# Eight of the 22 blocks of half 1's first feed-forward moved from beside half 0 to the head of half 1's own course

## The chip, the cores and the metric

One core of a Trainium2 chip runs the whole program. The time is device time in microseconds of one execution, as the median of several. A core has TensorE (PE, with its weight loads shown apart as PEld), VectorE (DVE), ScalarE (ACT), GpSimd (POOL) and SyncE (SP, which issues most DMAs here). Each engine takes its instructions in the order in which the program gives them to it.

## The reference, cut to what matters

Three transformer blocks follow each other on x of 512 tokens by 1024 channels, all in float32. What the change touches is the first step of the first block and the experts of the second:

```python
def first_block(x, ...):
    x = layer_norm(ALPHA * x + 0.5 * swiglu(x, ffn1_w_gate, ffn1_w_up, ffn1_w_down), ln1_g, ln1_b)
    # mixer: projections of x, HGRN2 over chunks, a causal convolution of width 31, output projection
    x = layer_norm(ALPHA * x + mix, ln2_g, ln2_b)
    x = layer_norm(ALPHA * x + 0.5 * swiglu(x, ffn2_w_gate, ffn2_w_up, ffn2_w_down), ln3_g, ln3_b)

def swiglu(x, w_gate, w_up, w_down):            # 1024 -> 2816 -> 1024
    return (silu(x @ w_gate) * (x @ w_up)) @ w_down

def second_block(x, ...):
    # mixer: spatial gating and a gated delta rule (a triangular solve per chunk of 64)
    ids, gates = peer_routing(h, wq, keys1, keys2)      # 8 heads x 16 experts for each token
    act = gelu(einsum('pd,phkd->phk', h, expert_u[ids]))
    x = x + gate * einsum('phk,phkd->pd', gates * act, expert_v[ids])
```

The third block (retention, a state space mixer and a feed-forward) comes last. The sequence is causal in the mixers, so tokens 256 to 511 need states of tokens 0 to 255, but not the other way round.

## The kernel before, in words

The tokens are worked on as two halves of 256 (`hf` 0 and 1, each two tiles of 128 tokens, `X(t)`). The program is written as one long course in which other work is mixed by hand.

- **Head** (`all`): half 0 goes through block 1 and the mixer of block 2 (`block1_first`, `layer_norm`, `block1_rest`, `mix2`). Here a weight tile (128x1024, 512 KB) is loaded by SP into `wr`, split by ACT (`wH`, L226) and DVE (`wL`, L227) into two parts, and each product is made of three matmuls. **Beside it runs the aside**: half 1's first feed-forward, a generator (`g_block1_first`), with its own tiles `fr`, `fH`, `fL` and `hH`, `hL`. Wherever the foreground is expected to leave PE without work it calls `idle(d)` with a fixed `GAP`, and pieces of the generator are issued for that long. `ASIDE1 = (4, 4, 4, 4, 4, 2)` says into how many parts its 22 blocks of 128 hidden channels are cut; a part of 4 takes 8 tiles of gate and up and 4 of down, one of 2 takes 4 and 2. `drain_side` issues what is left behind half 0's mixer.
- **Experts** (`experts`): now `exact` is true, a weight tile is used as it is in float32, and each product is one matmul (two records in the trace). `peer_route` makes half 0's expert ids, and its gathers go into the list `fill`: 512 steps that each fetch 128 rows of 4 KB by an indirect DMA of POOL (L1188) into one of 15 buffers `gu`; DVE makes a dot product of each row of `peer_u` (L1195), and a weighted sum of those of `peer_v` (L1218) that PE takes over in part (L1212). Some steps of the routing are in the list too. In front of this runs half 1's own course: `layer_norm` ln1, `block1_rest` (mixer 1 with hgrn and the convolution, ln2, second feed-forward, ln3) and `mix2`. Then half 1 is routed, and its gathers run beside half 0's block 3.
- **Tail** (`end`): half 1's block 3, with the rest of half 0's as aside.

How many gathers are issued beside the foreground is set by credit: each weight tile and each PSUM tile calls `tick(d, load)`, which adds `d * z * rate - load`, and a step is issued when its price (`DMA = 1.46` for a gather) is there. `z` is the first number of the stage's `ZONE`, the second (`vshare`) is the share of the weighted sums that PE takes. `course` sets the rate for a whole course from two fixed sums. At the second routing the list is emptied.

A float32 tile of the gate in this stage is issued so:

```python
raw = self.weight(self.wp, "w", 6 if self.exact else 4, src)      # wtile, L220: the DMA on SP
...
nc.tensor.matmul(ps[:, i * TH:(i + 1) * TH], a[:, k * P:(k + 1) * P], b[:, k, :], ...)   # g_fm, L280
```

`transpose_x` (L334) brings x into the layout that the matmuls take (`XH`, and `XL` when split); the down product is `g_tm` (L302 in float32, L304 to L306 split), whose result DVE adds to X (L390). In the delta recurrence of `mix2` a triangular inverse is built in steps: L1010 (PE), L1012 (ACT copy), L1016 and L1019 (PE), L1021 and L1022 (DVE subtractions).

Of the kernel before, what the change touches and what calls it, by code (L numbers as in the profile page):

```python
# [11 lines left out]
F32 = mybir.dt.float32  # L12
# [7 lines left out]
P = 128  # L20
T = 512
NT = 4
NH = 2
TH = 256
D = 1024
# [10 lines left out]
DMA, ROUTE, FINISH = 1.46, 0.8, 6.0  # L36
AHEAD = 8
GB = 15

ASIDE1 = (4, 4, 4, 4, 4, 2)  # L40
ASIDE3 = (4,) * 4
FIRST3 = 16
ADA = 28
CONV_PE = (0, 2)

ZONE = dict(x=(1, 0.5), g=(1, 0.35), h=(1.15, 0.41), c=(0.43, 0.4), f=(1.43, 0), m=(1.73, 0.06), d=(1.09, 0.4),
            R=(1.09, 0.39), r=(1.33, 0.3), F3=(1.1, 0), s=(1, 0.65))

GAP = dict(_0=4, l=3, h=0.74, c=0.22, m=5.53, d=0.9, r=0.5, s=1.6, _4=5.2, ln=8, l4=8)
# [1 line left out]
WEIGHTS = 3  # L51
# [26 lines left out]
class Ker:  # L78
# [68 lines left out]
    def course(self, i):  # L147

        whole, loads, share = COURSE[i]
        self.rate, self.credit = (share * sum(f[0] for f in self.fill) + loads) / whole, 0.0  # L150

    def tick(self, d, load=0.0):
# [11 lines left out]
    def zone(self, name):  # L164
        self.z, self.vshare = ZONE[name]

# [300 lines left out]
    def g_block1_first(self, parts):  # L467
        nc = self.nc
        yield from self.g_transpose_x(lambda t, k: self.X(t)[:, k * P:(k + 1) * P])
        for t in range(NH):  # L470
            self.aux.tensor_scalar(self.X(t), self.X(t), float(ALPHA), None, op0=ALU.mult)
        yield from self.g_ffn_glu("f1g", "f1u", "f1d", parts)

    def block1_rest(self):
        self.zone("g")
        self.mixer1()
        self.zone("f")
        self.layer_norm("ln2_g", "ln2_b", ALPHA)
        if self.hf == 0:
            self.fill, self.rate, self.credit = self.later, RATE_ADA[1], 0.0  # L480
        with self.tc.tile_pool(name="ada", bufs=1) as self.adap:
            self.ffn_glu("f2g", "f2u", "f2d", (22,))
            self.pop(9999 if self.hf == 0 else 0)
        self.layer_norm_out("ln3_g", "ln3_b")
# [1316 lines left out]
    def all(self, out):  # L1801
        tc = self.tc
        self.load_x()
        with ExitStack() as ef:
            self.wp = ef.enter_context(tc.tile_pool(name="wp", bufs=1))
            self.ff0 = ef.enter_context(tc.tile_pool(name="aside", bufs=1))
            with ExitStack() as es:
                self.xt(es)
                self.ff = self.ff0
                self.aside(1, lambda o: o.g_block1_first(ASIDE1))  # L1810
                ada = self.ada_setup()
# [20 lines left out]
    def experts(self, out):  # L1832


        tc = self.tc
        with ExitStack() as ep:
            self.exact = True
            self.wp = ep.enter_context(tc.tile_pool(name="wp", bufs=1))
            self.peer_open(ep)
            self.zone("x")  # L1840
            self.fill = []
            self.peer_route(RATE_ROUTE[0])
            self.course(0)
            self.hf = 1
            with ExitStack() as es:
                self.xt(es)
                self.layer_norm("ln1_g", "ln1_b", ALPHA)
                self.block1_rest()
            self.mix2()
            self.zone("R")  # L1850
            self.peer_route(RATE_ROUTE[1])
            self.course(1)
            self.hf = 0
            last = self.ctx.enter_context(ExitStack())
            with ExitStack() as es:
                self.xt(es)
                self.block3_mix()
                X = self.XH, self.XL
                self.exact = False
                self.xt(last, "right")  # L1860
                X3 = self.XH, self.XL
                self.exact = True
                self.XH, self.XL = X
                self.zone("F3")
                self.whole(self.g_norm3())
                for i in range(0, KD, 2):
                    i = slice(None), slice(i, i + 2)
                    self.fill_pair(self.XH[i], self.cut(X3, *i))
                self.whole(self.g_ffn_relu2((FIRST3,)))
            self.exact = False  # L1870
            self.XH, self.XL = X3
            self.rate = 0.0
            self.ff = last.enter_context(tc.tile_pool(name="aside3", bufs=1, side="right"))
            self.aside(0, lambda o: o.g_block3_last(out, ASIDE3, FIRST3), False)
            self.aux = self.nc.gpsimd
            self.next_piece()
            self.pop(9999)
# [149 lines left out]
```

## Time and profile before

| | us |
|---|---|
| median of 3 runs | 3463.89 (3454.16 to 3475.46) |
| the profiled execution | 3472.09 |
| its span, first to last instruction | 3470.3 |

| engine | busy us | share of the span |
|---|---|---|
| PE | 3035.7 | 87% |
| DVE | 2661.0 | 77% |
| POOL | 1437.0 | 41% |
| ACT | 1152.0 | 33% |

In all 956.97 MB are moved, 276 GB/s in the mean. The shares are averages over three quite different stretches: the head reaches to about 908 us, the experts from there to about 2896 us, the tail from there to the end. The mean granted clock of TensorE is 0.932 of full speed.

### The profile page before, as it was taken

What the parts mean: (1) busy time and instruction counts of PE and PEld (TensorE: products, weight loads), DVE (VectorE), ACT (ScalarE), POOL (GpSimd) and SP (SyncE); (2) the same over time, 40 slices, a digit from 0 to 9 for tenths busy, and PEclk for the clock granted to TensorE, in tenths of its full rate; (3) what the DMA queues carried; (4) which work ended last, traced back from release to release, by engine and by line L of the source; (5) the groups of instructions that cost most, each with busy time, mean ns of one, the idle gap of its engine ahead of it and who ended that gap; (6) DMA issues with size and microseconds to landing.
All of it is one profiled execution on the core that took longest, in us unless ns stands there. A gap on an engine that the chain in (4) does not pass through costs nothing. (4 is left out here: it accounts for less than half of the span.)

```text
span 3470.3 us, 44861 instructions
## 1 busy us (share of the span) xinstructions
PE 3035.7 (87%) x15418; PEld 2355.2 (68%) x15418; DVE 2661.0 (77%) x6451; ACT 1152.0 (33%) x1694; POOL 1437.0 (41%) x1187
## 2 busy tenths in 40 slices
PE   9999999998979789988677859798888975999998
PEld 9987889888866458846354644465644644888897
DVE  7779676665488999779898989898778776566655
ACT  4454544553312242103122121122222213455554
POOL 0020000023245656656677567667677671211200
PEclk9999999999989899998788979898899987999999
DMA  8863476542389979998989889999999995644364
GB/s 313 283 193 116 135 266 228 169 157 85 110 297 363 342 290 382 409 396 348 374 319 377 324 324 401 327 382 351 334 363 361 409 390 186 185 131 138 122 188 162
DMA packets 276469, 956.97 MB, mean 276 GB/s; under 512 B 38272, under 2 KB 41856, under 8 KB 276240
## 3 DMA queue, kind: packets, MB, share of 16 engines
q0 software_dynamic: 147456, 536.94, 40.9%
q1 hardware_dynamic: 128784, 417.16, 35.0%
q8 instruction: 122, 2.00, 0.2%
q14 instruction: 107, 0.88, 0.1%
HBM read 947.68 MB, written 2.10 MB: 274 GB/s over the span
## 5 line engine op out<-in xcount | busy, mean ns | idle before, releaser
L1188 POOL DMA_INDIRECT gu<-in_peer_u,idx x512 | 614.6, 1200 | 368.0 <-issue 114.1
L1188 POOL DMA_INDIRECT gu<-in_peer_v,idx x512 | 627.5, 1226 | 306.1 <-issue 112.3
L1195 DVE SCALAR_TENSOR_TENSOR gu<-gu 128x1024 f32<-128x1024 f32 x512 | 622.1, 1220 | 61.5 <-DMA gu<-in_peer_u,idx 60.7
L227 DVE TENSOR_TENSOR wL<-wr,wH 128x1024 fp32r<-128x1024 f32 x332 | 409.2, 1235 | 251.1 <-ACT wH L226 231.9
L280 PE MATMUL ps<-XH,wr 128*128 128x256 f32 x2368 | 535.8, 386 | 0.0
L280 PEld LDWEIGHTS ps<-XH,wr 128*128 128x128 f32 x2368 | 454.8, 194 | 72.1 <-issue 11.5
L226 ACT CAST wH<-wr 128x1024 fp32r<-128x1024 f32 x332 | 348.7, 1051 | 448.4 <-PE ps L305 219.5
L1218 DVE SCALAR_TENSOR_TENSOR gu<-gu,act 128x1024 f32<-128x1024 f32 x362 | 463.5, 1280 | 27.3 <-DMA gu<-in_peer_v,idx 21.6
L1212 PE MATMUL ps<-gu,dg 128*128 128x512 f32 x584 | 318.7, 672 | 95.1 <-DMA gu<-in_peer_v,idx 43.0
L1212 PEld LDWEIGHTS ps<-gu,dg 128*128 128x128 f32 x584 | 117.6, 214 | 212.5 <-issue 150.9
L302 PE MATMUL ps<-wr,XH 128*128 128x512 f32 x512 | 230.2, 602 | 0.0
L280 PE MATMUL ps<-XH,wH 128*128 128x256 f32 x1408 | 208.1, 290 | 13.2 <-ACT XH L138 11.2
L280 PE MATMUL ps<-XH,wL 128*128 128x256 f32 x1408 | 202.7, 288 | 3.2 <-DVE wL L227 3.0
L280 PE MATMUL ps<-XL,wH 128*128 128x256 f32 x1408 | 202.8, 288 | 0.2
L280 PEld LDWEIGHTS ps<-XH,wH 128*128 128x128 f32 x1408 | 187.9, 197 | 19.1 <-ACT XH L138 15.3
L280 PEld LDWEIGHTS ps<-XH,wL 128*128 128x128 f32 x1408 | 186.1, 196 | 4.7 <-DVE wL L227 4.6
L227 DVE TENSOR_TENSOR fL<-fr,fH 128x1024 fp32r<-128x1024 f32 x98 | 127.1, 1298 | 79.4 <-ACT fH L226 48.6
L280 PEld LDWEIGHTS ps<-XL,wH 128*128 128x128 f32 x1408 | 186.4, 197 | 0.6 <-DVE XL L140 0.6
L302 PEld LDWEIGHTS ps<-wr,XH 128*128 128x128 f32 x512 | 97.9, 194 | 121.5 <-issue 119.1
L226 ACT CAST fH<-fr 128x1024 fp32r<-128x1024 f32 x98 | 102.7, 1049 | 183.6 <-PE ps L280 57.7
L302 PE MATMUL ps<-wr,hH 128*128 128x512 f32 x304 | 135.4, 607 | 18.1 <-DVE xres L390 13.0
L208 POOL TENSOR_TENSOR r<-rx,mhalf 128x1 f32<-128x1 f32 x18 | 11.9, 668 | 335.9 <-DVE rx L206 332.5
(619 smaller groups left out, 5391.1 us busy)
## 6 DMA issues: line engine op xcount, KB each, us to landing
wr<-in_wi_fm SPq DMA_DIRECT2D x112, 512.0 KB
wr<-in_wi_tm SPq DMA_DIRECT2D x96, 512.0 KB
wr<-in_wf SPq DMA_DIRECT2D x96, 512.0 KB
wr<-in_wo SPq DMA_DIRECT2D x64, 512.0 KB
wa<-in_wada SPq DMA_DIRECT2D x48, 512.0 KB
wr<-in_f2g SPq DMA_DIRECT2D x44, 512.0 KB
wr<-in_f2u SPq DMA_DIRECT2D x44, 512.0 KB
wr<-in_f2d SPq DMA_DIRECT2D x44, 512.0 KB
```

Of the source, the lines that this page charges most:

```text
L208: nc.gpsimd.tensor_tensor(out=out, in0=x, in1=self.mhalf[:p, :].to_broadcast(list(out.shape)), op=ALU.pow)
L226: self.nc.scalar.copy(H, raw)
L227: self.nc.vector.tensor_tensor(out=L, in0=raw, in1=H, op=ALU.subtract)
L280: nc.tensor.matmul(ps[:, i * TH:(i + 1) * TH], a[:, k * P:(k + 1) * P], b[:, k, :], start=n == 0, stop=n == KD * len(terms) - 1)
L302: nc.tensor.matmul(pss[t], lh[:, ts], wh, start=k == 0, stop=k == nk - 1)
L1188: nc.gpsimd.indirect_dma_start(out=g, out_offset=None, in_=I[src], in_offset=bass.IndirectOffsetOnAxis(ap=idx[:, s:s + 1], axis=0))
L1195: nc.vector.scalar_tensor_tensor(g, g, 1.0, h2, op0=ALU.mult, op1=ALU.mult, accum_out=st["act"][:, s:s + 1])
L1212: nc.tensor.matmul(st["ps"][i], dg, g[:, i * 512:(i + 1) * 512], start="pe" not in st, stop=s == 127)
L1218: nc.vector.scalar_tensor_tensor(st["acc"], g, c, st["acc"], op0=ALU.mult, op1=ALU.add)
```

## The change

`ASIDE1` becomes `(4, 4, 4, 2)`: the aside makes 14 of half 1's 22 blocks. The other eight are made in one part at the head of half 1's course, ahead of ln1, in float32 as it is there and with the gathers beside them; the new zone `f1` has the numbers of the second feed-forward's. As the transposed x of half 1 is gone by then, x is fetched a second time and transposed again. The rate of the course is worked out with the added tiles.

```diff
-ASIDE1 = (4, 4, 4, 4, 4, 2)
+ASIDE1 = (4, 4, 4, 2)
...
+ZONE = dict(f1=(1.43, 0), x=(1, 0.5), g=(1, 0.35), h=(1.15, 0.41), c=(0.43, 0.4), f=(1.43, 0), ...
...
     def course(self, i):
         whole, loads, share = COURSE[i]
+        n = 2 * (FIRST3 - 16) if i else 3 * (22 - sum(ASIDE1))
+        whole, loads = whole + n * WEIGHTS, loads + n * DMA
         self.rate, self.credit = (share * sum(f[0] for f in self.fill) + loads) / whole, 0.0
...
+    def block1_more(self):
+        fb = sum(ASIDE1)
+        if fb == 22:
+            return
+        self.zone("f1")
+        with self.tc.tile_pool(name="xin", bufs=1) as xp:
+            xi = xp.tile([P, NH, D], F32, name="xi")
+            for t in range(NH):
+                self.nc.sync.dma_start(xi[:, t, :], self.I["x"][self.tg(t) * P:(self.tg(t) + 1) * P, :])
+            self.transpose_x(lambda t, k: xi[:, t, k * P:(k + 1) * P])
+        self.ffn_glu("f1g", "f1u", "f1d", (22 - fb,), fb)
+        self.zone("x")
...
                 self.xt(es)
+                self.block1_more()
                 self.layer_norm("ln1_g", "ln1_b", ALPHA)
                 self.block1_rest()
```

With `FIRST3 = 16` the rate of the second course stays as it is.

## Rows read from the trace of the kernel before

**Rows 1.** Busy time of the engines by stretch: PE, PEld, DVE, ACT, POOL, clock, DMA.

```profile
772.30:908.30 136.00, 124.23 (x919) 115.42 (x919) 74.20 (x109) 56.26 (x76) 40.41 (x30) 0.97 0.27 86
...
794.50:829.70 35.20, 34.99 (x258) 33.13 (x259) 18.12 (x25) 11.87 (x15) 6.38 (x5) 0.95 0.25 81
...
860.20:894.70 34.50, 34.50 (x247) 32.31 (x248) 17.15 (x21) 11.97 (x15) 6.44 (x5) 0.96 0.27 80
...
1125.00:1232.00 107.00, 82.10 (x303) 45.53 (x301) 101.31 (x307) 23.60 (x44) 73.47 (x64) 0.90 0.94 346
...
1448.00:1533.00 85.00, 79.94 (x225) 42.91 (x224) 56.09 (x131) 6.00 (x9) 50.99 (x42) 0.98 1.03 409
...
1693.00:1852.00 159.00, 111.61 (x559) 78.19 (x559) 146.43 (x291) 37.22 (x65) 114.30 (x96) 0.83 0.91 327
```

**Rows 2.** The same by stretch for tile fr alone: DVE and ACT, half 0's delta.

```profile
772.30:908.30 136.00, 30.20 (x23) 23.69 (x23) 0.97 0.27 86
```

**Rows 3.** The same for tile wr: a dense stretch of the second feed-forward, half 0.

```profile
592.00:638.00 46.00, 0.00 (x0) 0.00 (x0) 20.81 (x17) 17.24 (x17) 1.00 0.61 193
```

**Rows 4.** Order of time, half 0's delta, one step of the inverse: start, duration.

```profile
867.49 1.13 PE L1010 MATMUL ps<-xx,alv 128*128 128x128 f32 x8
...
870.89 1.23 DVE L227 TENSOR_TENSOR fL<-fr,fH 128x1024 fp32r<-128x1024 f32 x1 [0.16 <-ACT fH L226]
...
872.04 0.68 DVE L1021 TENSOR_TENSOR xx<-xx,ps 128x512 f32<-128x512 f32 x1
...
873.00 0.39 PE L1010 MATMUL ps<-xx,alv 128*128 128x128 f32 x2
```

**Rows 5.** Order of time, the same step for half 1 among the experts.

```profile
1745.59 1.05 PE L1010 MATMUL ps<-xx,alv 128*128 128x128 f32 x8
...
1749.32 0.49 PE L1010 MATMUL ps<-xx,alv 128*128 128x128 f32 x2
```

**Rows 6.** Order of time, half 0's delta, norm of k in the second chunk.

```profile
844.04 0.68 DVE L947 TENSOR_REDUCE ss<-osq 128x4 f32<-128x512 f32 x1
...
844.63 1.87 DVE L227 TENSOR_TENSOR fL<-fr,fH 128x1024 fp32r<-128x1024 f32 x1
...
846.43 0.16 DVE L206 TENSOR_SCALAR rx<-ss 128x4 f32<-128x4 f32 x1
```

**Rows 7.** Order of time, half 0's delta, PE around a wait.

```profile
791.05 0.40 PE L306 MATMUL ps<-fL,hH 128*128 128x512 f32 x1
...
794.45 0.95 PE L1003 MATMUL ps<-ident,xt 128*128 128x128 f32 x4 [3.00 <-POOL xt L1000]
...
795.05 0.77 PE L304 MATMUL ps<-fH,hH 128*128 128x512 f32 x1
```

**Rows 8.** Costliest groups, 1320 to 1533 us: busy, mean ns, idle before.

```profile
L280 PE MATMUL ps<-XH,wr 128*128 128x256 f32 x676 | 146.1, 379 | 0.0
...
L1195 DVE SCALAR_TENSOR_TENSOR gu<-gu 128x1024 f32<-128x1024 f32 x57 | 69.5, 1219 | 30.0 <-DMA gu<-in_peer_u,idx 29.9
...
L1218 DVE SCALAR_TENSOR_TENSOR gu<-gu,act 128x1024 f32<-128x1024 f32 x53 | 67.8, 1280 | 6.4 <-DMA gu<-in_peer_v,idx 5.1 <-issue 1.2
...
L302 PE MATMUL ps<-wr,hH 128*128 128x512 f32 x142 | 62.8, 604 | 5.1 <-DVE hH L416 5.1
```

**Rows 9.** Order of time on SP ahead of half 1's first layer norm.

```profile
1038.32 0.33 SPq L194 DMA_DIRECT2D gf<-in_ln_g_c  x1
```

**Rows 10.** Order of time on PE through half 1's first layer norm.

```profile
1040.95 1.94 PE L726 MATMUL ps<-ident,grc 128*128 128x128 f32 x8 [2.12 <-DVE gu L1195]
...
1047.66 1.88 PE L302 MATMUL ps<-wr,XH 128*128 128x512 f32 x4
```

**Rows 11.** Order of time on PE through half 1's second layer norm.

```profile
1301.51 1.88 PE L302 MATMUL ps<-wr,XH 128*128 128x512 f32 x4
...
1310.28 3.56 PE L334 MATMUL ps<-ident,xres 128*128 128x128 f32 x16 [5.15 <-DVE xres L369]
1313.67 1.68 PE L280 MATMUL ps<-XH,wr 128*128 128x256 f32 x7
```

More of the change, by code (lines that the diff above doesn't have):

```diff
@@ L44 @@
 CONV_PE = (0, 2)
-ZONE = dict(x=(1, 0.5), g=(1, 0.35), h=(1.15, 0.41), c=(0.43, 0.4), f=(1.43, 0), m=(1.73, 0.06), d=(1.09, 0.4),
+ZONE = dict(f1=(1.43, 0), x=(1, 0.5), g=(1, 0.35), h=(1.15, 0.41), c=(0.43, 0.4), f=(1.43, 0), m=(1.73, 0.06), d=(1.09, 0.4),
             R=(1.09, 0.39), r=(1.33, 0.3), F3=(1.1, 0), s=(1, 0.65))
```

## Prediction

> **What bounds the kernel now.** I read the page's slices first for the regimes, then one table of stages, then the order of time inside two of them. In the slices the reader is to see that PE is high and DMA low at the head and the tail of the span, and that DMA and DVE are high and PE has gaps in between, where the experts' gathers run. So the blocks are moved from a stretch with spare DMA to one with almost none.
>
> The stages show it in numbers [rows 1]. In the delta recurrence of half 0 (772 to 908 us) PE is busy 124 of 136 us, DVE 74, DMA 27%. In the experts' stages the limit changes: DVE 101 of 107 us in half 1's hgrn, DMA 1.03 with PE busy 80 of 85 us in the last third of its second feed-forward (1448 to 1533), DVE 146 of 159 us with DMA at 0.91 in its delta, at a granted clock of 0.83.
>
> Which work goes? The aside of half 1 takes its weight tiles in order, 66 of them. Parts of 4, 4, 4 and then 2 blocks use 42 tiles; the last 24 disappear. Before, 23 of the aside's tiles are rounded between 772.3 and 908.3 us [rows 2]; by the order of the aside's loads these are the ones that disappear (one more was rounded just ahead). Nothing ahead of 772 us changes but that two down tiles stand where two gate tiles stood. So the gain has one place, the delta recurrence of half 0.
>
> **Part 1: the delta recurrence without the aside.** One aside tile costs PE what any split tile costs: 17 tiles in 46.0 us where PE has nothing to wait for [rows 3], 2.71 us; 24 x 2.71 = 65 us is the most that can come back.
>
> How much does? I compare one step of the triangular inverse with and without it. With the aside a step lasts from 867.49 to 873.00, 5.51 us [rows 4]: the rounding of an aside tile occupies DVE from 870.89 for 1.23 us, the subtraction that the chain needs starts only at 872.04, and PE is never free. Half 1 runs the same step among the experts, with no aside: where little of the gathers comes between, it lasts from 1745.59 to 1749.32, 3.73 us [rows 5]. That is the bare chain of two matmul groups, a copy and a subtraction. There are two chunks; each has five full steps, a shorter sixth and a transpose ahead. I take 24.0 us for a bare chunk (5 x 3.73, and an estimated 5.4 for the rest, from the same rows). With the aside the two loops take 35.2 and 34.5 us [rows 1]. Gain in the loops: 69.7 - 48 = 22 us.
>
> Outside the loops lie 65 us, in which the chain goes through DVE, ACT and POOL, and the aside's casts and roundings stand in their queues. One place: the sum of squares is there at 844.72, the rounding holds DVE from 844.63 to 846.50, and the next link starts at 846.43 [rows 6]: 1.7 us. The same happens to squares behind casts on ACT and to POOL operations that DVE slows. I estimate 4 us per chunk for the norms, 3.5 for the mask chain and 1 at the end, 16 in all; bounds 6 and 20.
>
> Against this stands the clock. After 3.00 us without work PE's 512-column matmuls take 0.77 us where they took 0.40 [rows 7], so they run at 1.2 instead of 2.4 GHz for a while. Without the aside such waits become more: I expect some four of them, each with four more matmuls at 0.37 us longer, 1.5 us: -6. Gain: 22 + 16 - 6 = **32 us**, with 10 (the loops give nothing) and 65 as ends.
>
> The Trainium skill's page "TensorE: Matmul & The Clock Gate" (section "HAM oscillation — how this bites in real kernels") speaks against the change: a kernel that waits between short bursts of matmuls falls to the lower clock in each wait and pays in the burst behind it. If that held in each step of the inverse, the gain would be about 10 us, which is the rival below. The row after the 3.00 us wait agrees; no row shows it for the 0.7 us waits inside a step.
>
> **Part 2: the eight blocks beside the experts.** There a weight is used unsplit. The nearest rows are the second feed-forward of the same half, the same loop with the same zone (1.43, 0). From 1320 to 1533 us there are 676 records of the gate and up matmuls, 16 to a tile, and 142 of the down ones, 8 to a tile: 60 tiles in 213 us, 3.55 us each, and beside them DVE uses 57 + 53 gathers, 1.83 per tile [rows 8]. So 24 tiles take 85 us and use 44 gathers. DVE work per tile is that of the rows as well: all weighted sums on DVE, and routing steps among them.
>
> Around it: x is fetched again. Its two DMAs go where the layer norm's loads now are issued, at 1038.32 [rows 9], when the routing's tiles come free; the other SP entries behind are weights, six of which are fetched ahead anyway. PE stands idle before that point already and starts at 1040.95 on the rows that they bring [rows 10]; for 1 MB in place of a row I take 2 us more (bounds 0 and 5; who waits is PE, for the transposes). The 16 transposes are 3.6 us by those of a norm [rows 11], with their start 4. The layer norm itself was done early: its statistics lay in the routing stage, and on PE it takes 6.7 us (1040.95 to 1047.66 [rows 10]). Behind the new blocks it hangs on their last sum, as the second norm does: from the end of the output matmul at 1303.4 to the first gate matmul at 1313.67 are 10.3 us, 5.15 of them idle [rows 11]. That is +4. Together 85 + 2 + 4 + 4 = 95 us of course.
>
> What comes off: the number of gathers is fixed, so the 44 used here, and some 5 in the ten microseconds around, are missing elsewhere in the course. The code does that by its rate: 72 and 35 are added to the whole and the loads, and with some 746 units left in the list (480 gathers of 1.46, 42 routing steps of 0.8, two ends of 6) the rate falls from (0.895 x 746 + 189.8) / 822.9 = 1.04 to 1.00, which takes some 25 gathers out of the other stages; the rest is missing at the second routing, which drains what is left. What is one worth there? Where DMA is full, 0.524 MB at the 409 GB/s of the fullest stage [rows 1], 1.28 us; where DVE is, 1.22 us for a dot product and 1.28 for a weighted sum [rows 8], of which PE takes up to half, so about 1.0; where PE's chain is the limit, nothing. I take 1.1, as the stages are about half DVE and half DMA: 49 x 1.1 = 54 us. Cost: 95 - 54 = **41 us**. Ends: if every stage fills up with what it lacks, only the DVE work that is new remains (8 evictions and products of some 0.68 us, by L1021 of the same size [rows 4], and 9 weighted sums of 1.28 that were PE's): 17 us. If all is DMA, 26 transfers of 1.28 us: 33 us. If the other stages give back only a third: 95 - 18 = 77 us.
>
> **Sum.** -32 + 41 = +9 us. The profiled execution took 3472.09 us (span 3470.3 and 1.8 around it), 8.2 above the median of the three times, 3463.89; the difference carries over: 3463.9 + 9 = **3473 us**.
>
> **Rivals.**
> *PE is the bound of the delta stage and all comes back.* For it: PE busy 124 of 136 us there. Against: the step of 3.73 us and 65 us outside the loops where DVE, POOL and ACT set the pace. Then -65; with a price between the two lower ends of 17 and 33, 25 us, the sum is -40: 3424 us. What decides is whether the stage gives back over 60.
> *The delta stage falls to the lower clock.* Slower. The place is the inverse: the 0.7 us waits that the aside filled are open, and if they hold PE at 1.2 GHz, each of the two groups on the chain (1.05 us) takes 0.9 longer, and a step 5.5 us, what it takes now. The gain is then 10 and the sum +32; with a cost somewhat over mine, 50, +40: 3504 us. It decides when the granted clock of that stage is under about 0.65. Against it: half 1's delta stage has its waits and 0.83.
> *The experts' course is a sum, not a mix.* The other stages are held by their own chains (delta, the hgrn steps, norms), fewer gathers there leave gaps, and a third comes back: +77 - 32 = +45, 3509 us. For it: PE is idle for 48 of the delta's 159 us although gathers are at hand [rows 1]. Against: DMA at 1.0 in the feed-forward, DVE over 92% in hgrn and delta, which is what fewer gathers relieve.
> *The blocks don't really move* can't be: the source takes 24 tiles out of the aside. What could be is that the end of the aside was hidden and removing it frees nothing; that is the end of 10 us and part of the second rival.
>
> **How the numbers follow.** A measurement of this kernel tells about 1% from no change, 35 us. My forecast, a sum between -35 and +35, has 0.64. The first rival 0.12, all faster by more. The second has 0.11 and the third 0.13, both slower by more. So faster 0.12, same 0.64, slower 0.24. For 8 in 10 the range leaves half of the first rival and about half of the others out: 3436 to 3512 us.
>
> **What would show it.** Right: no rounding of aside tiles behind 772 us; half 0's delta stage near 104 us instead of 136; steps of about 3.8 us in its loops; then a stage of 24 unsplit tiles from about 1010 us on, 3.5 to 3.7 us each, DMA at 1.0; the first layer norm of half 1 behind it with about 5 us of idle PE; the rest of the first course some 50 us shorter in sum, a good part of it at the second routing; everything behind unchanged. Wrong: granted clock under 0.65 in the delta loops; the stage of the 24 tiles over 100 us; the later stages as long as now; or x landing late, with PE waiting for it for more than 5 us.

## The result and the profile after

The changed kernel takes 3556.81 us (four runs, 3554.81 to 3564.63), the kernel before 3463.80 beside it: a ratio of 1.0272, 95% interval 1.0253 to 1.0291. It is 93 us slower, where 9 were forecast and 3512 us was the top of the range. The profiled execution of the changed kernel took 3564.63 us, with a span of 3562.9; against the 3470.3 of before that is +92.6. Line numbers are up to 16 higher after.

Two loads of SP mark where half 0's block 3 begins (cos) and where the tail begins (rw). What runs from the end of the first routing to cos is called the first course here, what runs from cos to rw the second. Before:

```profile
2039.67 0.33 SPq L194 DMA_DIRECT2D cos<-in_c_cos  x1
...
2897.14 0.43 SPq L194 DMA_DIRECT2D rw<-in_ret_norm_w  x1
```

After:

```profile
2146.34 0.33 SPq L196 DMA_DIRECT2D cos<-in_c_cos  x1
...
2989.14 0.43 SPq L196 DMA_DIRECT2D rw<-in_ret_norm_w  x1
```

PE in order of time through the added stage after, from the transposes of the x fetched again to the first matmul behind ln1:

```profile
1020.46 3.80 PE L336 MATMUL ps<-ident,xi 128*128 128x128 f32 x16 [19.41 <-DVE gu L1211]
1024.10 55.42 PE L282 MATMUL ps<-XH,wr 128*128 128x256 f32 x256
...
1096.13 4.26 PE L304 MATMUL ps<-wr,hH 128*128 128x512 f32 x6 [6.31 <-DVE hH L418]
...
1114.82 3.60 PE L1228 MATMUL ps<-gu,dg 128*128 128x512 f32 x8
1121.24 1.06 PE L742 MATMUL ps<-ident,grc 128*128 128x128 f32 x8 [2.82 <-DMA grc<-in_ln_g_c]
...
1136.38 3.74 PE L1228 MATMUL ps<-gu,dg 128*128 128x512 f32 x4 [5.65 <-DMA gu<-in_peer_v,idx]
...
1142.14 1.12 PE L304 MATMUL ps<-wr,XH 128*128 128x512 f32 x2
```

With [rows 10] this gives the account. At PE's first work behind the first routing the changed kernel is 20.5 us ahead (1020.46 against 1040.95), at the first matmul behind ln1 94.5 late (1142.14 against 1047.66): **the added stage costs 115 us, not 95**. At cos it is 106.7 late: **the rest of the first course, which was to give 54 back, takes 12 more**. At rw it is 92.0 late: the second course, with block 3 of half 0, takes 14.7 less. The tail adds 0.6.

Stretches after (columns as in [rows 1]): half 0's delta stage; the 24 tiles; ln1; the down tiles of the second feed-forward; ln3.

```profile
770.20:894.90 124.70, 88.51 (x521) 76.14 (x520) 41.40 (x81) 24.97 (x42) 35.88 (x31) 0.84 0.02 6
...
1024.10:1115.00 90.90, 84.59 (x323) 61.49 (x322) 78.01 (x212) 13.12 (x17) 56.40 (x46) 0.96 1.03 405
1115.00:1142.10 27.10, 16.73 (x60) 8.54 (x59) 26.82 (x85) 6.91 (x16) 20.43 (x18) 0.87 0.99 369
...
1553.80:1632.00 78.20, 78.20 (x235) 43.10 (x234) 14.05 (x30) 3.80 (x7) 5.62 (x6) 1.00 0.64 208
1632.00:1707.60 75.60, 34.89 (x115) 22.30 (x114) 65.49 (x132) 12.07 (x20) 53.35 (x46) 0.73 0.94 356
```

The first row runs from the load of PM to that of half 0's last down tiles of the mixer; between the same two loads before lie 144.4 us at a clock of 0.98. So the delta stage gives back 19.7 us, and its clock has fallen to 0.84. Inside it the step of the inverse is as forecast, 3.89 us, and the waits outside the loops are there too, with matmuls at half speed behind them (2.08 us for eight records that take 1.13 later):

```profile
793.47 1.12 PE L1019 MATMUL ps<-ident,xt 128*128 128x128 f32 x4 [3.98 <-POOL xt L1016]
795.26 2.08 PE L1026 MATMUL ps<-xx,alv 128*128 128x128 f32 x8 [0.67 <-ACT xx L1020]
...
809.80 1.13 PE L1026 MATMUL ps<-xx,alv 128*128 128x128 f32 x8
811.66 1.16 PE L1032 MATMUL ps<-pw,xt 128*128 128x128 f32 x8 [0.73 <-ACT pw L1028]
...
813.69 1.13 PE L1026 MATMUL ps<-xx,alv 128*128 128x128 f32 x8
```

The row that speaks loudest is that of the second feed-forward's 44 gate and up tiles in the costliest groups after, 1417.5 to 1571.2 us:

```profile
L282 PE MATMUL ps<-XH,wr 128*128 128x256 f32 x704 | 153.1, 381 | 0.0
```

With 69 gathers beside it a record takes 381 ns and PE never waits; in [rows 8], with 110 beside 60 tiles, it took 379 and never waited either. And in the last down tiles, where hardly a gather ran (DMA at 0.64, six issues on POOL), 72 records take 31.06 us, 3.45 us a tile (shown with late_finish). So of the 3.55 us of a tile, in a stretch that the prediction took to be full by DMA, about 3.45 are PE's own.

### The profile page after: what moved, and what is told of

Same layout as the page of the kernel before. It is cut to its first block, busy times and chain, and to the rows that moved or that the text cites. A ratio compares the mean times of both kernels' runs of the same rounds, so it can differ in the third digit from the quotient of the medians.

```text
span 3562.9 us, 44413 instructions
## 1 busy us (share of the span) xinstructions
PE 3048.7 (86%) x15238; PEld 2360.0 (66%) x15238; DVE 2638.7 (74%) x6428; ACT 1111.7 (31%) x1653; POOL 1429.3 (40%) x1187
## 5 line engine op out<-in xcount | busy, mean ns | idle before, releaser
L282 PE MATMUL ps<-XH,wr 128*128 128x256 f32 x2624 | 594.1, 386 | 2.8 <-issue 2.7
L282 PEld LDWEIGHTS ps<-XH,wr 128*128 128x128 f32 x2624 | 504.9, 194 | 82.3 <-issue 13.9
L1234 DVE SCALAR_TENSOR_TENSOR gu<-gu,act 128x1024 f32<-128x1024 f32 x371 | 475.2, 1281 | 37.4 <-DMA gu<-in_peer_v,idx 35.5
L1228 PE MATMUL ps<-gu,dg 128*128 128x512 f32 x548 | 283.3, 647 | 92.2 <-DMA gu<-in_peer_v,idx 84.3
L1228 PEld LDWEIGHTS ps<-gu,dg 128*128 128x128 f32 x548 | 108.5, 209 | 201.0 <-issue 178.8
L304 PE MATMUL ps<-wr,hH 128*128 128x512 f32 x368 | 163.1, 604 | 6.3 <-DVE hH L418 6.3
L1226 ACT ACTIVATE dg<-ident,act 128x128 f32<-128x128 f32 x137 | 52.9, 399 | 291.3 <-PE ps L1228 248.3
L1343 DVE SCALAR_TENSOR_TENSOR rt<-io,rt 128x50 f32<-128x50 f32 x512 | 135.4, 264 | 10.1 <-remote 4.0
```

The lines of the kernel that those rows point to most:

```text
L304: nc.tensor.matmul(pss[t], lh[:, ts], wh, start=k == 0, stop=k == nk - 1)
L1226: nc.scalar.activation(dg, self.ident, AF.Copy, scale=c)
L1228: nc.tensor.matmul(st["ps"][i], dg, g[:, i * 512:(i + 1) * 512], start="pe" not in st, stop=s == 127)
L1234: nc.vector.scalar_tensor_tensor(st["acc"], g, c, st["acc"], op0=ALU.mult, op1=ALU.add)
L1343: nc.vector.scalar_tensor_tensor(st["jk"], io, st["fp"][:, h, k:k + 1], st["cid"][:, h, :], op0=ALU.is_equal, op1=ALU.mult, accum_out=st[" ...
```

## The experiments

Theory **sum**: in the tile loops PE sets the pace, elsewhere the stages' own chains do; a gather that goes missing leaves a gap and saves next to nothing. Rival **mix**, as predicted: DMA or DVE is the bound and a gather that goes missing saves 1.1 us. More theories came up on the way. The sixteen runs were made in four sets, with 3462, 3474, 3442 and 3442 us for the kernel before beside them. So times are told as ratios within a set, with the 95% interval in brackets, and behind it as that ratio's share of 3464 us. Lengths out of traces can be compared across sets in the first course: from E, a load of SP at its start, to PM, the load ahead of half 1's delta, they are 651.2 us in the kernel before and 650.8 in before_524, which is of another set. The second course lasts 820 to 867 us in the sixteen traces, and no run explains most of that.

**head_only**: the aside cut, nothing in its place.

```diff
     def block1_more(self):
+        return
...
     def course(self, i):
...
-        n = 2 * (FIRST3 - 16) if i else 3 * (22 - sum(ASIDE1))
+        n = 2 * (FIRST3 - 16) if i else 0
```

> The aside of 14 blocks, and the other eight blocks are left out altogether (no second load of x, the rate of the course as before). The prediction's first term: -32 us, 3432. The traces of before and after, where the delta stage of half 0 went from 144.4 to 124.7 us and everything up to the second routing lies 17 to 22 us earlier: -17 to -20, 3445. If the end of the aside had been all of PE's bound: -65, 3399.

Ratio 0.9949 (0.9927 to 0.9971), -18 us. The head is worth what the two traces said, not 32 and not 65. The remaining 112 us of the change lie in the added stage and behind it.

**late_finish**. After, DVE stands still for 31 us at half 0's first finishing step, which adds PE's share of the sums (L1244). PE reaches that share only behind the 72 records of down tiles:

```profile
1570.83 31.06 PE L304 MATMUL ps<-wr,hH 128*128 128x512 f32 x72
1601.73 1.88 PE L1228 MATMUL ps<-gu,dg 128*128 128x512 f32 x4
...
1602.79 0.69 DVE L1244 TENSOR_TENSOR gu<-ps,gu 128x512 f32<-128x512 f32 x1 [31.00 <-PE ps L1228]
...
1694.21 3.86 PE L336 MATMUL ps<-ident,xn 128*128 128x128 f32 x16 [34.88 <-issue]
```

```diff
-        self.fill = u + [...] + b[16:20] + last[16:] + b[20:]
+        k = 48 if self.hf == 0 else 20
+        self.fill = u + [...] + b[16:k] + last[16:] + b[k:]
```

> The changed kernel, with the finishing step of half 0's first tile put 28 steps further back in the list, so that it falls behind ln3 as in the kernel before, and not among the last down tiles of the second feed-forward. Theory of the finishing step (DVE waits 31 us for PE there, the gathers stand still, and pile up in ln3): ln3's stage goes from 75.6 back to about 53 us, -15 to -22, 3535 to 3542. Rival (the 34.9 us wait in ln3 comes from the gathers among its own DVE steps and stays): within 5 us of 3557.

Ratio 1.0226 (1.0194 to 1.0257), +78, so 16 us better than the changed kernel. But only part of it is where it was expected. The long wait of ln3 shrinks from 34.88 to 14.22 us:

```profile
1682.18 1.12 PE L336 MATMUL ps<-ident,xn 128*128 128x128 f32 x4 [14.22 <-ACT xn L762]
```

PE reaches this point 12.0 us earlier, yet cos only 2.2 earlier. That the gathers which now run in the down tiles and behind ln3 take most of it back is argued, not shown. The rest of the gain lies in the second course. So the misplaced step is a small part of the 93 us.

**few_gathers** and **few_gathers96** measure the price of a gather: 48 or 96 of half 0's 512 are left out of the kernel before, and the rate follows.

```diff
+        if self.hf == 0:        # few_gathers; in few_gathers96: o[2] % 16 in (0, 5, 10, 15)
+            order = [o for o in order if o[2] < 96 or o[2] % 16 not in (1, 3, 5, 7, 9, 11)]
```

> The kernel before, with 24 of the 256 gathers of each of half 0's two tiles left out (12 of 128 experts), 48 in all, 43 of them out of the first course, spread evenly by the rate; nothing else changes. It measures what the prediction priced at 1.1 us a gather. Mix, as predicted: 43 x 1.1 = -47 us, about 3417. Sum (PE sets the pace in the tile loops and its chains elsewhere, a gather that is missing leaves a gap): a quarter of that at most, -5 to -12, about 3455.

> The kernel before, with 48 of the 256 gathers of each of half 0's two tiles left out (24 of 128 experts), 96 in all, spread by the rate (0.91); twice the dose of few_gathers, at which the first course, from the end of the first routing to block 3 of half 0, lasted 995.8 us against 997.2. Mix, as predicted: 85 x 1.1 = -94 us in the first course, 3370 to 3380 at the end. Chains and PE set the pace, and missing gathers leave gaps: 0 to -25 in the first course; the second one starts with 524 steps left as in few_drained, which was worth 20 there: 3430 to 3470.

few_gathers: 1.0036 (1.0019 to 1.0053), +12 us. Its first course, between these two loads of SP, is 996.2 us long; before, it ran from 1042.02 to 2039.67, 997.7 us:

```profile
1042.45 0.91 SPq L561 DMA_DIRECT2D E<-in_lb_logits  x2
...
2038.69 0.33 SPq L194 DMA_DIRECT2D cos<-in_c_cos  x1
```

The 43 gathers that this course lacks save 1.4 us, 0.03 each; the +12 at the end lie behind it. few_gathers96: 0.9922 (0.9905 to 0.9939), -27. Its first course, between the same two loads, is 966.8 us long:

```profile
1039.88 0.91 SPq L561 DMA_DIRECT2D E<-in_lb_logits  x2
...
2006.70 0.33 SPq L194 DMA_DIRECT2D cos<-in_c_cos  x1
```

That is 30.9 us less, 0.36 for each of the 85 gathers that are missing there: a third of 1.1. The mix falls, since it asked for -47 and -94; but "nothing comes back" holds at the smaller dose alone.

**few_drained**, **keep_rate_late**, **before_fast**: is it only the gathers drained at the second routing (issued there because the list is emptied) that cost? few_drained keeps the rate and leaves the 48 out. keep_rate_late is the changed kernel at the rate of before. before_fast is the kernel before with a higher share. In all three the finishing step stays behind ln3.

```diff
     def course(self, i):                      # few_drained
+        left = sum(f[0] for f in self.fill) + (0 if i else 48 * DMA)
-        self.rate, ... = (share * sum(f[0] for f in self.fill) + loads) / whole, 0.0
+        self.rate, ... = (share * left + loads) / whole, 0.0
...
-COURSE = ((822.8886, 189.8, 0.895), ...)      # before_fast
+COURSE = ((822.8886, 189.8, 0.96), ...)
```

> The same 48 gathers of half 0 left out of the kernel before as in few_gathers, but the rate of the course stays at 1.06, so that the stages keep their gathers and nearly all the missing ones are missing at the second routing (35 drained there in place of 73); half 0's first finishing step stays behind ln3. Theory that only a drained gather has a price: 38 x 0.83 = -32 us up to the end of the second routing, 3425 to 3440. Rival, a gather is worth the same everywhere (few_gathers: nothing): 3462 to 3475.

> The changed kernel with the rate of the course left at 1.06 (no share for the added tiles), so that 32 gathers are drained at the second routing in place of 62, and with the finishing step behind ln3. Theory of the drain: 30 x 0.83 = -25 us against late_finish, about 3514. Mix, where DMA or DVE is the bound in the stages: no more than 5 us against late_finish, since the gathers only change their place.

> The kernel before, its aside of 22 blocks unchanged, with the share of the first course at 0.96 in place of 0.895 and the finishing step 24 steps further back, so that it stays behind ln3: 49 gathers are drained at the second routing in place of 73, the other 24 lie in the stages. Theory of the drain: 24 x 0.83 = -20 us, 3442. Mix: DMA is at 1.00 and 1.03 in the second feed-forward, 24 x 1.1 come back there as longer stages: 3460 to 3470.

few_drained: 0.9942 (0.9920 to 0.9964), -20 us, but cos comes at 2037.10, 2.6 earlier only, and not 32; so the -20 lie in the second course and price no gather. keep_rate_late: 1.0291 (1.0263 to 1.0318), +101, no better than the changed kernel and 23 us worse than late_finish. before_fast: 1.0122 (1.0094 to 1.0150), +42. The theory of the drain falls, and the mix did not foresee this either: with some 24 gathers moved into the stages, before_fast takes 46 us longer up to half 1's delta (PM's load at 1739.0 in place of 1693.2), and the second routing gets no shorter. PE, whose shares of the sums stand in its order, now waits for rows that come late. PE in before_fast:

```profile
1725.76 2.04 PE L1213 MATMUL ps<-gu,dg 128*128 128x512 f32 x2 [17.85 <-issue]
...
2034.69 2.05 PE L1213 MATMUL ps<-gu,dg 128*128 128x512 f32 x2 [28.27 <-DMA gu<-in_peer_v,idx]
```

That would be 2 us for each, but it is not a price: in keep_rate_late 26 more gathers than in late_finish are issued between E and PM (385 against 359), and that stretch is 3.0 us longer (790.9 against 787.9); from E to cos it is 10. About the same number of gathers costs 46 us in one kernel and 3 in the other. What sets the difference is not shown; PE's waits above point to the place where a share of the sums falls, more than to the number of gathers.

**f1_no_gathers**: the zone f1 at 0.479.

> The changed kernel, with the zone f1 at 0.479, so that no gather is issued beside the 24 tiles; they are issued later, some 40 more, a third of them at the second routing. Mix (the 3.55 us of a tile are DMA's, 1.28 for the weight and 1.83 x 1.28 for the gathers): the 24 tiles go from 91 to 65 us or less (2.71 as a split tile). Sum (3.45 us of a tile are PE's own): they stay at 83 to 85 us, only the 6.3 us wait and a part of ln1's 27 us go; at the end 3557 -20 + 15 to 35 for the drained gathers, 3552 to 3572.

Ratio 1.0444 (1.0412 to 1.0476), +154, outside both. The change did not do what it was to do: although the credit asks for none, POOL issues 44 gathers beside the tiles (1021 to 1114 us), which were asked for elsewhere in the program. The gate and up records take 379 ns as ever:

```profile
L282 PE MATMUL ps<-XH,wr 128*128 128x256 f32 x256 | 55.4, 379 | 0.0
...
L1204 POOL DMA_INDIRECT gu<-in_peer_v,idx x22 | 27.2, 1235 | 21.7 <-DVE rt L1343 7.0 <-DVE gu L1211 6.6 <-issue 3.4
L1204 POOL DMA_INDIRECT gu<-in_peer_u,idx x22 | 24.2, 1100 | 21.3 <-DVE gu L1211 6.3 <-DVE gu L1234 5.6 <-issue 3.4
```

cos comes at 2181.2, 35 us later than in the changed kernel, although both reach half 1's delta at the same time (1805.2 and 1807.5). Here the added gathers at the second routing do cost: 94 are issued from the load of keys to cos, 31 more than in the changed kernel, and that stretch is 32 us longer (183.7 against 151.7). As a test of the tiles without gathers it fails; bare_after makes that test.

**two_blocks**: ASIDE1 = (4, 4, 4, 4, 4), 6 tiles moved.

> The changed kernel with ASIDE1 = (4, 4, 4, 4, 4): two blocks, 6 tiles, are moved in place of eight, 24 tiles. It parts what a moved tile costs from what the move costs once (x, transposes, the norm behind a feed-forward). Sum: 6 x 3.5 = 21, + 4 for the transposes, + 17 to 20 for ln1 and up to 6 for the wait at the hidden tile, less 4 at the head, 0 to -15 behind: +30 to +45, 3493 to 3508. The terms of the prediction: 6 x 3.55 + 10 - 12 x 1.1 - 8 = +10, 3474.

Ratio 1.0185 (1.0161 to 1.0208), +64, above both: a quarter of the tiles costs two thirds of the whole. The stage itself costs no more than the sum has for it: PE's first matmul behind ln1 comes 34.6 us late. Behind it the course loses 32 more, about 9 of them in hgrn, where PE waits 23.9 us for DVE; before, the longest wait in this place was 11.0, at the step ahead of it, and for ACT. PE in two_blocks:

```profile
1082.23 1.98 PE L304 MATMUL ps<-wr,XH 128*128 128x512 f32 x4
...
1202.54 1.83 PE L671 MATMUL ps<-E 128*128 128x128 f32 x7 [23.93 <-DVE E L667]
```

**quiet_ln1** gives ln1 a zone (0, 0). **before_524** issues ten more steps at the second routing: `self.pop(10)` behind `peer_route`.

> The changed kernel with zone (0, 0) in half 1's first layer norm: its ticks issue no gathers and PE takes no weighted sums there. It asks what stretches this norm from the 6.7 us of before to 27.1 us. Gathers asked for there: the norm falls to 15 to 20 us and the time by 7 to 12, 3545 to 3550. DVE's backlog from the routing and from the tiles ahead (DVE reaches the last sum only 9 us after PE): it stays at 25 us or more, 3553 to 3560.

> The kernel before with one change: ten more steps of the list are issued at the end of the second routing, so that the second course starts with 524 steps left and a rate of 2.016, as in the changed kernel, late_finish and few_drained, where it lasted 842, 820 and 832 us, against 857 before. Theory that this gives the second course its 15 us in the changed kernel: -10 to -20, 3443 to 3455. Rival, that it is the order in which the first list left things: within 5 us of the kernel before.

quiet_ln1: 1.0276 (1.0249 to 1.0303), no gain. From the last down tile to the first matmul behind the norm PE still takes 33.0 us (1096.8 to 1129.8). But the norm was not emptied: POOL issues 21 gathers in that time, DVE makes 15 dot products and sums, and PE 22 records of its share (13.2 us); after, in 27.1 us, they were 18, 17 and 24 (13.0 us). So what runs in the norm was asked for elsewhere, and as a test of a norm without it this run fails, like f1_no_gathers; bare_after makes that test. before_524: 0.9988 (0.9977 to 0.9998), -4 us: nothing to build on, and no cause of the shorter second course. Its second course lasts 822.5 us in the trace, 35 less than in the trace of before, which is from another set; its second routing is 10 longer, and against the kernel before of its own set it gains 4 at the end. So the 15 us of the changed kernel can be a difference between sets; that stays open.

**after_warm** fills PE's waits in half 0's delta with matmuls that nobody reads.

```diff
+    def warm(self, n):
+        if self.hf == 0 and not self.exact and self.side is None:
+            ps = self.ps.tile([P, 512], F32, tag="ps", name="ps")
+            for _ in range(n):
+                self.nc.tensor.matmul(ps[:, :P], self.ident, self.ident)
```

> The changed kernel with filler matmuls of 128 columns, whose result nobody reads, in half 0's delta recurrence at the places where PE waits: ten ahead of the transposes of q, twelve ahead of the inverse, two in each step behind the copy, nine ahead of the head norm. It asks what the lower granted clock (0.84 of full speed in this stage) takes of the 32 us that were expected there. Clock: the granted clock rises to 0.95 or more and the stage falls from 124.7 to 112 to 118 us, 3545 to 3550. Chains through DVE, ACT and POOL: the clock rises, the stage stays at 122 to 128 us, the time within 5 us.

```profile
762.60:876.50 113.90, 94.90 (x693) 84.06 (x693) 41.20 (x81) 24.91 (x42) 35.89 (x31) 0.98 0.02 7
```

The clock is back at 0.98 and the stage lasts 113.9 us. On the same chip, in quiet_ln1, it takes 124.7 at 0.84 as in the changed kernel, with DVE, ACT and POOL as busy:

```profile
759.30:884.00 124.70, 88.52 (x521) 76.09 (x520) 41.37 (x81) 24.98 (x42) 35.90 (x31) 0.84 0.02 6
```

So the clock cost 10.8 us. The ratio at the end is 1.0255 (1.0238 to 1.0272), 7 us below quiet_ln1's, but the two intervals overlap: a gain at the end is not shown.

**bare_before**, **bare_after**, **no_fetch**, **small_dve** take half 0's gathers away, whole or in part, with the list's steps and pace kept.

```diff
+            if h0 and s not in (0, 127):       # in fetch, bare_*; no_fetch: return self.gs, a tile loaded once
+                return None                    # u_step and v_step do nothing with None
...
+            n = slice(0, 32 if h0 else D)      # small_dve: dot products and sums over 32 columns
```

> The kernel before without 504 of half 0's 512 gathers, and without their dot products and weighted sums; the list keeps its steps and its pace, so that all else stands where it stood. It shows what the stages of the first course last by themselves. PE and chains set the pace: the tile loops stay as they are (second feed-forward 131.3 and about 80 us, projections 77), hgrn, delta and the two routings get shorter by the gathers' DVE work; the first course falls from 997 to 850 to 900, 3320 to 3370 at the end. Mix: the tile loops fall too, to 2.71 us a tile as for split ones (179 in place of 211 us for the 66 tiles of the second feed-forward); the first course falls to 750 to 800, 3210 to 3270.

> The same for the changed kernel. The difference to bare_before is the price of the move with no gathers beside it. PE's own time: 24 x 3.46 + 4 for the transposes + 10 for a norm behind a feed-forward - 7 as before - 20 at the head = +70. Mix: 24 x 2.71 + 7 - 20 = +52. What the changed kernel costs beyond the difference (93 - 70) is then what the gathers do with the added stage, in place of the 54 that they were to give back.

> The kernel before, half 0's gathers left out but not what is done with them: dot products and sums read one tile that stays (14 buffers in place of 15). DVE's and PE's part is as before, DMA's is gone. If the transfers hold the stages: near bare_before. If DVE does: within 30 us of the kernel before.

> The kernel before with all gathers, but half 0's dot products and DVE's weighted sums over 32 of the 1024 columns; PE's share is as before. If DVE's work holds the stages: near bare_before. If the transfers do: within 30 us of the kernel before.

bare_before: 0.9587 (0.9569 to 0.9605), -143 us, between the two forecasts; 504 gathers with all that is done with them are worth 0.28 us each. The decisive row is that of the 44 gate and up tiles of the second feed-forward (1255 to 1468 us):

```profile
L280 PE MATMUL ps<-XH,wr 128*128 128x256 f32 x704 | 152.2, 379 | 0.0
```

With no gather at all the record takes the same 379 ns. From the load of ln2's gf to the last f2d, which brackets this feed-forward, 240.1 us of before become 233.3. What gets shorter is hgrn and the convolution (234.9 to 195.8 us from the load of cb to that of gf), ln3 with the mixer's projections (165.7 to 141.0), delta (185.8 to 151.1, up to the second load of keys) and the second routing (160.7 to 129.8).

bare_after: 0.9731 (0.9715 to 0.9748), so **the move costs 51 us with no gathers beside it** (3349.47 less 3298.87). PE there, at ln1:

```profile
1079.63 4.03 PE L304 MATMUL ps<-wr,hH 128*128 128x512 f32 x9
1086.31 1.94 PE L742 MATMUL ps<-ident,grc 128*128 128x128 f32 x8 [2.65 <-DMA grc<-in_ln_g_c]
...
1091.81 1.45 PE L304 MATMUL ps<-wr,XH 128*128 128x512 f32 x3
```

The 24 tiles take 82.9 us (1000.77 to 1083.66), 3.45 each, and the norm 8.2, not 27.1. The wait for hH is gone as well. The stretch of the tiles:

```profile
1000.80:1083.70 82.90, 82.86 (x321) 60.59 (x320) 76.97 (x664) 17.96 (x25) 5.63 (x6) 1.00 0.61 189
```

no_fetch: 0.9933 (0.9914 to 0.9953), -23 us; small_dve: 0.9906 (0.9876 to 0.9936), -33. Taken singly, transfers and DVE's work give 56 of the 143 us; neither is *the* bound of this course. Two readings of the other 87 us stand. Either part alone may hold most of what both hold. Or they are PE's: bare_before also leaves out PE's share of the sums, which no_fetch keeps (196 records from the tile that stays, 99.7 us of PE) and small_dve too. No run takes away that share alone, so how the 87 us divide is not shown.

## Why the prediction was wrong

**Where the change acts** was right: no rounding of an aside tile is left behind 772 us, the 24 tiles stand from 1024 us on, 46 gathers are issued beside them where 44 were forecast, and x costs PE nothing to speak of (it starts 20.5 us earlier, where the head gives 19.7).

**Part 1**, 32 us: the sign and the mechanism were right, the size 1.6 times too high; it measured 19.7 in the trace and 18 in head_only. Of the two gains, 22 + 16 = 38, 30.5 are there at full clock (144.4 to 113.9, in a run that has its fillers in it). The term that was mis-sized most in proportion is the clock, "four waits ... 1.5 us: -6". It is 10.8, where the granted clock fell to 0.84, not near 0.65. The waits of 3 to 4 us outside the loops carry it; inside the loops the granted clock recovers, and the step of 3.89 us at full speed disproves the second rival. The Trainium skill's page "TensorE: Matmul & The Clock Gate" (section "HAM oscillation — how this bites in real kernels"), which stood beside that rival, tells of a kernel whose waits for DMA end each time in a burst at the lower clock. The trace agrees for the wait of 3.98 us (2.08 us for what takes 1.13 later); the waits of 0.73 us in a step, which are far shorter than those of the page's kernel, are followed by full speed.

**Part 2, the course**, 95 us: 115 were measured. The tiles were right, 3.52 us each for 3.55, once the 6.3 us wait for hH is taken off. The norm was not. The prediction took "the second norm" [rows 11], 10.3 us, as the model, but that one stands behind an output projection. The norm behind a feed-forward is ln3, and its row was in the trace of before: from the end of the last down tile at 1548.06 to the next transposes at 1573.72 lie 25.7 us.

```profile
1531.59 16.47 PE L302 MATMUL ps<-wr,hH 128*128 128x512 f32 x38
...
1573.72 1.12 PE L334 MATMUL ps<-ident,xn 128*128 128x128 f32 x4 [13.60 <-ACT xn L746]
```

ln1 after takes 27.1. DVE is behind: it reaches the last sum of the new blocks at 1123.68, where PE had the product at 1114.99, and among the norm's small steps stand dot products and sums of 1.22 and 1.28 us. PE's own share of the sums stands there too, 24 records of 13.0 us. bare_after (8.2 us) shows that it is the gathers' work, on DVE and PE together; quiet_ln1 shows that the norm's own ticks did not ask for it.

**The step that failed is "What is one worth there? ... I take 1.1"**, the relief of 54 us. It rests on "where DMA is full", read from a DMA share of 1.03 in the second feed-forward [rows 1]. In the same stretch PE's groups had 0.0 and 5.1 us of idle time [rows 8]: PE was full as well, and an unsplit tile costs it 3.45 us with or without gathers (few_gathers, bare_before). Two full resources were taken for one. The other stages gave hardly any back in the kernel before for 43 gathers (0.03 us each) and 0.36 each for 85. In the changed kernel the second routing got 9.4 us shorter with 17 gathers fewer (keys to cos, 151.7 against 161.1), but the stages ahead of it took 21.6 longer. So where 54 us were to come back, 12 were lost. The third rival had the right sign; its "a third comes back" holds for 85 gathers, but not for 43, nor for the changed kernel, and with its own +45 it was 48 us short. Its argument, gaps in the stages that their chains hold, is borne out by few_gathers.

Of the 84 us between +9 and +93, 66 are this step, 20 the added stage (the norm above all), 12 the head, and the second course takes 14 off.

**What the gathers did instead.** Without them the move adds 46.9 us to the span (3342.8 less 3295.9), with them 92.6. Of the 46 us between, 27 lie in the added stage: 19 in ln1 (27.1 against 8.2), 6 in the wait for hH, 2 in the tiles. Another 7 lie ahead of it, where bare_after starts 27.8 us earlier than bare_before and the changed kernel 20.5. From the first matmul behind ln1 to cos the changed kernel loses 12 us, while bare_after gains 10 on bare_before: 22. In the second course 10 come off again. The finishing step among the down tiles is seen in ln3, but putting it back gains only 2.2 us at cos (late_finish), so it is next to nothing of the 22. For these only the place is shown, hgrn above all; that DVE comes to it with more in its queue is argued from two_blocks' wait of 23.9 us and not shown. Why the second course is 15 us shorter stays open too.

The first rival (all 65 come back) fell with head_only; that the blocks move was never in doubt.

## What to carry to other kernels

Before a transfer is called the bound of a stretch, read the idle time of the engine beside it in the same rows: where PE's group showed 0.0 idle, its own duration set the pace, and taking away half 0's gathers left its records at 379 ns. Price relief and load by experiment, in both directions and at more than one dose: here 43 gathers left out of a course gave 1.4 us and 85 gave 31, and some 25 put into the stages cost 46 us in one kernel and 3 in another. Look in the trace whether the edit emptied the place that it was to empty: two of these runs did not. And take the row for a moved step from a place with the same predecessor: a norm behind a feed-forward is another thing than one behind a projection.

## What the runs showed of the hardware that was not expected

The granted clock could be bought back with work that nobody reads: 113.9 us at 0.98 against 124.7 at 0.84 for the same chain, with 6.4 us more of busy PE. An unsplit float32 tile takes PE 3.45 us (379 ns a record) at DMA shares from 0.61 to 1.03. And a step of the list that is asked for in one stage can run in another: with no credit for gathers beside the 24 tiles, 44 of them still ran there.
